# Two neighbouring rows of the second expert matrix in each partition, and the inner values turned in that order

## The chip, the cores and the metric

The kernel runs on one core of a Trainium2 chip. A core has TensorE (PE in the profile, with its weight loads counted apart as PEld), VectorE (DVE), ScalarE (ACT), GpSimd (POOL), SyncE (SP, which here only issues DMAs) and 16 DMA engines that move data between HBM and SBUF. The metric is the device time of one execution in microseconds (us). Before the change it is 1613.43 us, the median of 3 runs (1612.79 to 1615.95).

## The reference

One decoder block over 512 tokens of width 1024. A convolution mixer and a forgetting-attention mixer run side by side, then comes a mixture of 32 experts, of which each token takes 4. All weights are float32. The change touches the experts only; for one expert `e` and its block of up to 128 tokens `xi` the reference computes

```python
hc = xi @ w1[e] + b1[e]                       # w1[e]: 1024 x 2048
g, u = hc[:, :D_EXPERT], hc[:, D_EXPERT:]     # D_EXPERT = 1024
g = jnp.minimum(g, SWIGLU_LIMIT)
u = jnp.clip(u, -SWIGLU_LIMIT, SWIGLU_LIMIT)
hm = (u + 1.0) * (g * jax.nn.sigmoid(SWIGLU_ALPHA * g))   # the inner values
return hm @ w2[e] + b2[e]                     # w2[e]: 1024 x 1024
```

The product `hm @ w2[e]` is a sum over the 1024 inner values. The order in which they are taken is free, as long as `hm` and `w2` are taken in the same one.

## The kernel before

The first 480 us or so hold the mixers, the router and the ranking of the experts. Then the 32 experts are worked through in order of their token counts, in pairs: an even position `p` is a "big" expert (up to 128 rows of tokens), an odd one a "small" expert (up to 64 rows, `small(p)`, line 247). Each expert needs 8 tiles of `w1` and 4 of `w2`, and each tile is one DMA of 1 MB into 128 partitions of 8 KB, issued from SP in `slot` (lines 197 to 244). A `w1` tile is 128 rows of the matrix, one row of 8 KB to a partition (line 232). A `w2` tile is 256 rows of 4 KB, two to a partition (lines 238 to 240): partition `q` of tile `j` holds row `256*j + q` in its first half and row `256*j + 128 + q` in its second.

Seven buffers receive these tiles in turn (line 1079). A raw tile `w` is split into two float32r parts (`split`, line 1306): ACT copies it to `wh`, which rounds it, and DVE subtracts to give `wl`. Four buffers hold such parts, and `split_to` (line 1299) makes them up to three steps ahead of TensorE (`AHEAD`, line 37). A raw buffer is free for the next DMA when its `wl` has been made. Two of a small expert's eight `w1` tiles (`whole`, line 250) are used in float32 without a split.

The order of the work is written out in `steps` (line 1284): the `w1` tiles of expert `p` with the `w2` tiles of expert `p - 1` between them. While `pinned[0]` is set, every instruction of PE, ACT and DVE that goes through the wrappers of line 55 keeps the order of the program, so nearly all of them carry the line L55 and are told apart by their tiles.

For the second product `turn_h` (line 1235) turns the inner values `sg_u` (tokens in partitions) into `hmh` and `hml` (inner values in partitions). It makes 8 transposes on TensorE for each expert: a block of 128 columns of `sg_u` is loaded as the weights, and the identity is streamed past it, into the PSUM tile `pz`. ACT and DVE then split `pz`. In `mm_w2` (line 1352) block `kk = 2*k + cc` is the left operand for half `cc` of tile `k`, into the PSUM tile `py`:

```python
for cc in range(2):
    kk = 2 * k + cc
    for n in range(2):
        o = cc * D + n * 512
        MM(PSY[p][:, n * 512:n * 512 + 512], l[:, kk, :], r[:, o:o + 512],
```

For a small expert ACT copies the lower half of `py` into `b1s` when its last `w2` tile is done (`y_out`, line 1265), and TensorE adds it to the upper half with the matrix `shift` a little later (`y_low`, line 1269). The gates, the scatter into `x1d` and the final norm follow; the last expert has its own ending, with the bias rows (`bias_rows`, line 1387).

Of the kernel before, what the change touches and what calls it, by code (L numbers as in the profile page):

```python
# [19 lines left out]
P = 128  # L20
# [25 lines left out]
def hybrid_block(ctx, tc, x, c, w_ada, b_ada, norm1_g, w_in, b_forget, conv_w, conv_b, conv_ln_g,  # L46
# [5 lines left out]
    def in_order(f):  # L52

        def g(*args, **kw):
            ins = f(*args, **kw)  # L55
            return tc.keep_in_program_order(ins) if pinned[0] else ins
        return g

    MM = in_order(nc.tensor.matmul)
    TR = in_order(nc.tensor.transpose)  # L60
# [27 lines left out]
    def f32(ap):  # L88
        return ap.bitcast(F32)
# [4 lines left out]
    ident = K.tile([P, P], F32, name="ident")  # L94
# [86 lines left out]
    def raw_slot(dt=F32):  # L181
        t = pools[count[0] % len(pools)].tile([P, 2048], dt, name="w", tag="w")
        count[0] += 1
        return t
# [3 lines left out]
    def expert(p):  # L188

        if p == 0:  # L190
            return slice(0, 1)
        if p not in numbers:
            numbers[p] = nc.values_load(permi[0:1, p:p + 1], engines=[mybir.EngineType.SP], min_val=0, max_val=NE - 1,
                                        skip_runtime_bounds_check_because="an expert's number")
        return bass.ds(numbers[p], 1)

    def slot(*key):

        if key in slot_tiles:
            return slot_tiles[key]  # L200
        kind = key[0]
        dma = nc.sync.dma_start
        if kind == "ada" and key[1]:
            t = AD.tile([P, 2048], F32, name="adaw", tag="w")

            def dma(dst, src):
                tc.keep_in_program_order(nc.sync.dma_start(dst, src))
        else:
            t = raw_slot()
        if kind in COL:  # L210
            v = t.rearrange("p (c f) -> p c f", c=KC)
            c0 = COL[kind] + 256 * key[1]
            nc.sync.dma_start(v, w_in_v[:, :, c0:c0 + 256])
        elif kind == "ada":
            if key[1] < 2:
                v = t
                dma(v, w_ada[key[2] * P:(key[2] + 1) * P, 2048 * key[1]:2048 * (key[1] + 1)])
            else:
                v = t.rearrange("p (c f) -> p c f", c=2)
                dma(v, w_ada[2 * key[2] * P:2 * (key[2] + 1) * P, D * (key[1] + 2):D * (key[1] + 3)]  # L220
                    .rearrange("(c p) f -> p c f", p=P))
        elif kind in ("co", "ao"):
            src = (w_conv_out if kind == "co" else w_attn_out).rearrange("(c p) f -> p c f", p=P)
            v = t[:, :1024].rearrange("p (c f) -> p c f", c=4)
            nc.sync.dma_start(v, src[:, :, 256 * key[1]:256 * (key[1] + 1)])
        elif kind == "wo":
            v = t.rearrange("p (c f) -> p c f", c=4)
            nc.sync.dma_start(v, w_out[512 * key[2]:512 * (key[2] + 1), 512 * key[1]:512 * (key[1] + 1)]
                              .rearrange("(c p) f -> p c f", p=P))
        elif kind == "w1":  # L230
            v = t
            d = nc.sync.dma_start(v, w1[expert(key[1]), key[2] * P:(key[2] + 1) * P, :]
                                  .rearrange("o p f -> p (o f)"))
            if key[1] == 0 and key[2] >= 7:
                tc.keep_in_program_order(d)
        else:
            v = t
            d = nc.sync.dma_start(t.rearrange("p (c f) -> p c f", c=2),
                                  w2[expert(key[1]), 256 * key[2]:256 * (key[2] + 1)]
                                  .rearrange("o (c p) f -> p (o c) f", p=P))  # L240
            if key[1] == 0:
                tc.keep_in_program_order(d)
        slot_tiles[key] = v
        return v


    def small(p):
        return p % 2 == 1
# [11 lines left out]
    with ExitStack() as fx:  # L260
# [6 lines left out]
        def bank(name):  # L267
            return PS.tile([P, 512], F32, name=name, tag="b")
# [30 lines left out]
        def ada_acc(pc, k):  # L299
            w = slot("ada", pc, k)  # L300
            if pc > 1 and k == 0:
                acc[pc] = page([P, D], F32, "acc")
            for i in range(2):
                if pc < 2:
                    wi, o, kk, new = w[:, i * D:(i + 1) * D], acc[i], k, k == 0
                else:
                    wi, o, kk, new = w[:, i, :], acc[pc], 2 * k + i, k == 0 and i == 0
                if pc:
                    ACT(o if new else wi, wi, AF.Copy, scale=cs[:, kk:kk + 1])
                    if not new:  # L310
                        nc.gpsimd.tensor_tensor(o, o, wi, op=OP.add)  # L311
                elif new:
                    TS(o, wi, cs[:, kk:kk + 1], None, op0=OP.mult)
                else:
                    STT(o, wi, cs[:, kk:kk + 1], o, op0=OP.mult, op1=OP.add)
# [14 lines left out]
        def split_next():  # L330
            if not order:
                return
            key, half = order.pop(0)
            raw = slot(*key)[:, :, half * P:(half + 1) * P]
            kc = raw.shape[1]
            hi = G.tile([P, kc, P], F32R, name="gh", tag="gh")
            lo = G.tile([P, kc, P], F32R, name="gl", tag="gl")
            ACT(hi, raw, AF.Copy)
            TT(lo, raw, f32(hi), op=OP.subtract)
            ready[key, half] = (hi, lo)  # L340
# [155 lines left out]
        def split_v(hf):  # L496
            vh = pages(2, [P, 4, 260], F32R, "vh")
            vl = pages(2, [P, 4, 260], F32R, "vl")
            for q4 in range(2):
                ks = slice(4 * q4, 4 * q4 + 4)  # L500
                raw = slot("v", hf)[:, ks, :]
                fr = wf[:, ks, 4 * hf:4 * hf + 4]
                ACT(vh[q4][:, :, 256:260], fr, AF.Copy)
                TT(vl[q4][:, :, 256:260], fr, f32(vh[q4][:, :, 256:260]), op=OP.subtract)
                ACT(vh[q4][:, :, 0:256], raw, AF.Copy)
                TT(vl[q4][:, :, 0:256], raw, f32(vh[q4][:, :, 0:256]), op=OP.subtract)
            return vh, vl
# [27 lines left out]
        for hf in range(2):  # L535
            vh, vl = vs[hf]
            for b in range(NB):
                ts = slice(b * P, (b + 1) * P)
                ps = bank("pvv")
# [240 lines left out]
        def oproj(i, which, ah, al):  # L780
            hi, lo = split_of((which, i // 2), i % 2)
            ps = bank("po")
            run(three(ps, lambda k: hi[:, k, :], lambda k: lo[:, k, :],
                      lambda k: hk(ah, k), lambda k: hk(al, k), 4))
            return ps
# [102 lines left out]
        for i in range(KC):  # L888
# [3 lines left out]
            ps = oproj(i, "co", aH, aL)  # L892
# [179 lines left out]
    with ExitStack() as ex:  # L1072
# [110 lines left out]
        def rows(p):  # L1183
            return HALF if small(p) else P
# [34 lines left out]
        HT, HM, PSH, PSY = {}, {}, {}, {}  # L1219

        def swiglu(p):
# [10 lines left out]
            TS(u, u, LIMIT + 1.0, 1.0 - LIMIT, op0=OP.min, op1=OP.max)  # L1232
            STT(u, s, TOP, u, op0=OP.min, op1=OP.mult)

        def turn_h(p):


            r = rows(p)
            if small(p):
                if p < NE - 1:  # L1240
                    t = X.tile([P, KC, P], F32R, name="hmh", bufs=1)
                else:
                    t = G.tile([P, KC, P], F32R, name="hmh", tag="gh")
                ps = bank("pz")
                for k in range(KC):
                    TR(ps[:, k * r:(k + 1) * r], HM[p][:r, k * P:(k + 1) * P], ident[:r, :r])
                ps3 = ps.rearrange("p (k q) -> p k q", k=KC)
                ACT(t[:, :, 0:r], ps3, AF.Copy)
                TT(t[:, :, r:P], ps3, f32(t[:, :, 0:r]), op=OP.subtract)
                HT[p] = t  # L1250
                return
            hi = X.tile([P, KC, P], F32R, name="hmh", bufs=1)
            lo = X.tile([P, KC, P], F32R, name="hml", bufs=1)
            for hf in range(2):
                ps = bank("pz")
                for k in range(4):
                    kk = 4 * hf + k
                    TR(ps[:, k * P:(k + 1) * P], HM[p][:, kk * P:(kk + 1) * P], ident)
                ps3 = ps.rearrange("p (k q) -> p k q", k=4)
                ks = slice(4 * hf, 4 * hf + 4)  # L1260
                ACT(hi[:, ks, :], ps3, AF.Copy)
                TT(lo[:, ks, :], ps3, f32(hi[:, ks, :]), op=OP.subtract)
            HT[p] = (hi, lo)
# [182 lines left out]
        for i, (kind, p, k) in enumerate(steps):  # L1446
# [3 lines left out]
            if kind == "w1":  # L1450
# [35 lines left out]
                if k == 1 and p >= 1:  # L1486
                    turn_h(p - 1)
# [20 lines left out]
            else:  # L1508
# [13 lines left out]
                if (p, k) == (NE - 2, 3):  # L1522
                    turn_h(NE - 1)
# [204 lines left out]
```

## Time and profile before

| | |
|---|---|
| median of 3 runs | 1613.43 us (1612.79 to 1615.95) |
| profiled execution, its own time | 1611.79 us |
| its span | 1610.0 us |
| PE busy | 1488.9 us (92%) |
| DVE busy | 1349.4 us (84%) |
| ACT busy | 1043.4 us (65%) |
| DMA queue of SP (q1) | 461.93 MB, 72.9% of 16 engines |

The span runs from the first instruction to the last; the execution's own time is 1.79 us longer. Busy shares are means over stages with different limits, so the stage of the experts has to be read apart from the mixers. A row of waits gives the engine, what it was about to make, what it waited for, the total in us, how many times and the longest. An idle time in the timeline stands in brackets with what ended it.

### The profile page before, as it was taken

How to read it: one execution, taken by the hardware profiler on the slowest of the kernel's cores; microseconds unless marked ns; L12 is line 12 of the kernel's file. 1: busy time of each engine (PE TensorE's matmuls, PEld its weight loads, DVE VectorE, ACT ScalarE, POOL GpSimd, SP SyncE). 2: the span in 40 equal slices, each digit the busy share in tenths (PEclk: the TensorE clock that was granted, in tenths of full speed). 3: DMA queues.
4: the chain of work that ended last, by engine and by line, in shares of the span. 5: the costliest groups of instructions: out<-in, count | busy, mean ns of one | idle time of the engine just before them, and what ended most of it. 6: DMA issues, size and time to landing. Idle time of an engine off the chain costs nothing.

```text
span 1610.0 us, 18694 instructions
## 1 busy us (share of the span) xinstructions
PE 1488.9 (92%) x6626; PEld 1126.6 (70%) x6626; DVE 1349.4 (84%) x1282; ACT 1043.4 (65%) x953; POOL 406.6 (25%) x200
## 2 busy tenths in 40 slices
PE   2998999999967999999999999999999999999975
PEld 2776667778755777777777777777777777777743
DVE  6799998743676798898988989989898898988874
ACT  3534764522354777777777777877777777777671
POOL 0323341300131032231322313223222232222630
PEclk9997999989988999999999999999999999999987
DMA  8623342343557799999999999999999999999963
GB/s 321 208 79 105 103 132 99 124 144 95 206 196 258 312 362 400 389 407 406 394 392 407 390 404 368 404 384 408 389 391 393 399 390 402 385 386 373 405 243 114
DMA packets 115647, 489.81 MB, mean 304 GB/s; under 512 B 12983, under 2 KB 35627, under 8 KB 80728
## 3 DMA queue, kind: packets, MB, share of 16 engines
q1 hardware_dynamic: 103088, 461.93, 72.9%
q0 software_dynamic: 9200, 24.21, 5.4%
q10 hardware_dynamic: 3256, 2.39, 0.5%
q8 instruction: 54, 0.88, 0.2%
q14 instruction: 49, 0.40, 0.1%
HBM read 477.66 MB, written 18.63 MB: 308 GB/s over the span
## 4 chain that ended last, share of the span: by engine, by line
PE 55%; DVE 5%; ACT 4%; DMA 3%; issue 2%; POOL 0%; DVEq 0%; ACTq 0%
PE ph L55 37%; PE py L55 14%; DVE wl L55 3%; DMA w<-in_w_exp_in_dram 3%; ACT wh L55 3%; PE pz L55 2%; PE px L55 1%; ACT b1s L55 1%; ACT sg_u L55 1%; PE pi L55 1%; DMA xg<-in_b_exp_out_dram 0%; DVE w L55 0%; DVE sg_u L55 0%; DVE x L55 0%; DVE b1s L55 0%
## 5 line engine op out<-in xcount | busy, mean ns | idle before, releaser
L55 DVE TENSOR_TENSOR wl<-w,wh 128x2048 fp32r<-128x2048 f32 x352 | 796.5, 2282 | 89.5 <-ACT wh L55 86.2
L55 ACT ACTIVATE wh<-w 128x2048 fp32r<-128x2048 f32 x352 | 664.6, 1913 | 139.1 <-DMA w<-in_w_exp_out_dram 44.6
L55 PE MATMUL ph<-wh,xT 128*128 128x512 f32 x1408 | 377.0, 405 | 2.0 <-ACT sg_u L55 2.0
L55 PEld LDWEIGHTS ph<-wh,xT 128*128 128x128 f32 x1408 | 261.2, 190 | 72.3 <-issue 12.6
L1280 POOL DMA_INDIRECT x1d<-y,dstx x31 | 182.2, 5879 | 333.4 <-DVE y L55 333.4
L55 PE MATMUL ph<-wl,xT 128*128 128x512 f32 x896 | 241.6, 392 | 0.0
L55 PEld LDWEIGHTS ph<-wl,xT 128*128 128x128 f32 x896 | 169.1, 189 | 36.5
L55 PE MATMUL py<-wh,hmh 128*128 128x512 f32 x496 | 144.1, 412 | 1.3 <-DVE hmh L55 1.3
L55 PE MATMUL py<-wl,hmh 128*128 128x512 f32 x496 | 133.2, 390 | 0.2 <-DVE wl L55 0.2
L55 DVE SCALAR_TENSOR_TENSOR cacc<-apad,cw,cacc 128x512 f32<-128x512 f32 x120 | 117.3, 990 | 1.2
L55 PE MATMUL ph<-w,xT 128*128 128x512 f32 x256 | 115.2, 593 | 0.0
L311 POOL TENSOR_TENSOR acc<-acc,adaw 128x1024 f32<-128x1024 f32 x28 | 72.7, 2600 | 162.1 <-ACT adaw L55 156.2
L55 PEld LDWEIGHTS py<-wh,hmh 128*128 128x128 f32 x496 | 89.7, 188 | 31.9 <-issue 12.7
L55 PEld LDWEIGHTS py<-wl,hmh 128*128 128x128 f32 x496 | 93.0, 188 | 20.5 <-DVE wl L55 0.7
L55 ACT ACTIVATE gh<-w 128x1024 fp32r<-128x1024 f32 (+1 forms) x48 | 43.8, 914 | 87.6 <-PE zg L55 35.1
L1190 POOL MEMSET xg<- 64x1024 f32 (+1 forms) x31 | 29.6, 958 | 275.3 <-PE px L55 275.3
L1191 POOL DMA_INDIRECT xg<-h2d,dstx x31 | 65.6, 2116 | 117.5 <-DVE gat L55 103.0
L55 DVE TENSOR_TENSOR gl<-w,gh 128x1024 fp32r<-128x1024 f32 (+1 forms) x48 | 60.3, 1257 | 37.5 <-ACT gh L55 37.2
L55 PEld LDWEIGHTS ph<-w,xT 128*128 128x128 f32 x256 | 46.3, 190 | 46.1 <-issue 45.9
L55 ACT ACTIVATE xT<-px 128x512 fp32r<-128x512 f32 x50 | 29.7, 595 | 61.4 <-PE px L55 57.7
L55 PE MATMUL py<-wh,hml 128*128 128x512 f32 x256 | 68.6, 390 | 0.0
L55 ACT ACTIVATE sg_s<-ph 128x1024 f32<-128x1024 f32 (+1 forms) x32 | 32.8, 1024 | 44.3 <-PE ph L55 43.9
(379 smaller groups left out, 2106.6 us busy)
## 6 DMA issues: line engine op xcount, KB each, us to landing
w<-in_w_exp_in_dram SPq DMA_DIRECT2D x256, 1024.0 KB, 9.7
w<-in_w_exp_out_dram SPq DMA_DIRECT2D x128, 1024.0 KB, 12.4
w<-in_w_in_dram SPq DMA_DIRECT2D x18, 1024.0 KB, 5.6
adaw<-in_w_ada_dram SPq DMA_DIRECT2D x16, 1024.0 KB, 7.4
w<-in_w_ada_dram SPq DMA_DIRECT2D x8, 1024.0 KB, 6.8
w<-in_w_out_dram SPq DMA_DIRECT2D x4, 1024.0 KB
x<-in_x_dram SPq DMA_DIRECT2D x4, 512.0 KB
w<-in_w_attn_out_dram SPq DMA_DIRECT2D x4, 512.0 KB, 3.4
```

The costliest lines, as they stand in the source:

```text
L55: ins = f(*args, **kw)
L311: nc.gpsimd.tensor_tensor(o, o, wi, op=OP.add)
L1190: nc.gpsimd.memset(xgs[p][:r], 0.0)
L1191: nc.gpsimd.indirect_dma_start(out=xgs[p][:r], out_offset=None, in_=h2d[:, :], in_offset=bass.IndirectOffsetOnAxis(ap=dstx[:r, p:p + 1], a ...
L1280: nc.gpsimd.indirect_dma_start(out=x1d[:, :], out_offset=bass.IndirectOffsetOnAxis(ap=dstx[:r, p:p + 1], axis=0), in_=y, in_offset=None, b ...
```

## The change

A `w2` tile is read in another order: partition `q` of tile `j` now holds rows `256*j + 2*q` and `256*j + 2*q + 1`, which lie next to each other in HBM. The two pieces of 4 KB for a partition become one of 8 KB. So that the second product still pairs inner value and row, the block of `sg_u` that is turned as block `kk` is no longer 128 neighbouring columns but every second column of 256, starting at the even or the odd one.

```diff
@@ slot
             d = nc.sync.dma_start(t.rearrange("p (c f) -> p c f", c=2),
                                   w2[expert(key[1]), 256 * key[2]:256 * (key[2] + 1)]
-                                  .rearrange("o (c p) f -> p (o c) f", p=P))
+                                  .rearrange("o (p c) f -> p (o c) f", c=2))
@@ ahead of turn_h
+        def w2_rows(kk):
+
+            return slice(2 * P * (kk // 2) + kk % 2, 2 * P * (kk // 2 + 1), 2)
@@ turn_h, small expert
-                    TR(ps[:, k * r:(k + 1) * r], HM[p][:r, k * P:(k + 1) * P], ident[:r, :r])
+                    TR(ps[:, k * r:(k + 1) * r], HM[p][:r, w2_rows(k)], ident[:r, :r])
@@ turn_h, big expert
-                    TR(ps[:, k * P:(k + 1) * P], HM[p][:, kk * P:(kk + 1) * P], ident)
+                    TR(ps[:, k * P:(k + 1) * P], HM[p][:, w2_rows(kk)], ident)
```

No instruction is added or taken away, and none changes its place: PE, DVE, ACT, POOL and SP have the same instructions in the same order. On SP 127 rows of the listing read otherwise, the loads of `w2`, which have the form 128x2048 now (that of a `w1` load) where they had 128x2x1024.

## Rows read from the trace of the kernel before

**Rows 1.** The page: busy time of TensorE, the span in 40 slices with the granted clock and the DMA engines' share (tenths), and the count of DMA packets.

```profile
PE 1488.9 (92%) x6626; PEld 1126.6 (70%) x6626; DVE 1349.4 (84%) x1282; ACT 1043.4 (65%) x953; POOL 406.6 (25%) x200
...
PE   2998999999967999999999999999999999999975
...
PEclk9997999989988999999999999999999999999987
DMA  8623342343557799999999999999999999999963
...
DMA packets 115647, 489.81 MB, mean 304 GB/s; under 512 B 12983, under 2 KB 35627, under 8 KB 80728
```

**Rows 2.** Busy time of each engine in stretches of the stage of the experts (us from the span's start; busy us and number of instructions for PE, PEld, DVE, ACT, POOL; then the granted clock, the share of the DMA engines and GB/s).

```profile
600.00:700.00 100.00, 98.98 (x434) 74.83 (x434) 88.61 (x57) 76.83 (x53) 23.23 (x11) 1.00 1.00 396
700.00:800.00 100.00, 97.96 (x431) 73.18 (x430) 92.48 (x61) 74.99 (x52) 25.36 (x12) 1.00 1.01 400
...
1400.00:1500.00 100.00, 98.98 (x432) 74.32 (x431) 87.12 (x57) 76.62 (x53) 21.15 (x11) 1.00 0.97 384
```

**Rows 3.** Waits in the stretch from 600 to 1500 us: all of PE's, the DMA waits of ACT, and the longest of SP's queue.

```profile
PE py L55 <- ACT b1s L55: 13.2, 13, 1.0
...
ACT wh L55 <- DMA w<-in_w_exp_out_dram: 44.4, 34, 2.7
...
ACT wh L55 <- DMA w<-in_w_exp_in_dram: 24.7, 37, 2.3
...
SPq L232 <- DVE wl L55: 362.6, 154, 6.0
SPq L238 <- DVE wl L55: 144.0, 59, 3.1
```

**Rows 4.** The timeline from 719 us, around one of PE's waits (start, us, engine, line, operation, tiles, shape, count, idle time before).

```profile
719.25 1.03 ACT L55 ACTIVATE sg_s<-ph 128x1024 f32<-128x1024 f32 x1 [2.82 <-PE ph L55]
...
720.18 1.02 ACT L55 ACTIVATE sg_u<-ph 128x1024 f32<-128x1024 f32 x1
...
721.08 3.73 ACT L55 ACTIVATE wh<-w 128x2048 fp32r<-128x2048 f32 x2
...
724.83 1.02 ACT L55 ACTIVATE b1s<-py 64x1024 fp32r<-64x1024 f32 x1
...
725.90 0.73 PE L55 MATMUL py<-b1s,shift 64*128 64x512 f32 x2 [1.02 <-ACT b1s L55]
```

**Rows 5.** The page's median time from issue to landing of a tile of each matrix, and two stretches of 8 us, the first with loads of `w1` alone in flight, the second with loads of `w2` alone (columns as in Rows 2).

```profile
w<-in_w_exp_in_dram SPq DMA_DIRECT2D x256, 1024.0 KB, 9.7
w<-in_w_exp_out_dram SPq DMA_DIRECT2D x128, 1024.0 KB, 12.4
...
542.00:550.00 8.00, 8.00 (x37) 6.38 (x36) 5.23 (x4) 4.20 (x3) 0.96 (x1) 1.00 1.01 428
1539.00:1547.00 8.00, 8.00 (x30) 5.21 (x29) 8.00 (x5) 5.10 (x3) 8.00 (x1) 1.00 1.00 355
```

**Rows 6.** What SP spends on issuing one load, from 600 to 1500 us (ns, least, median and most; line 238 loads `w2`, line 232 `w1`).

```profile
L238 SPq DMA_DIRECT2D w<-in_w_exp_out_dram x108: 383/384/471, 599.9 to 1488.4; - x108
...
L232 SPq DMA_DIRECT2D w<-in_w_exp_in_dram x216: 332/333/690, 601.5 to 1499.1; - x108
```

**Rows 7.** Groups of weight loads on PE with their mean ns: those of the transposes of `sg_u` (the change is in these), those of the transposes of the tokens `xg`, one that loads 32 columns, one of an ordinary float32 product and the slowest of the list.

```profile
L55 PEld LDWEIGHTS pz<-ident,sg_u 128*128 128x128 f32 x128 | 14.9, 140 | 2.1
...
L55 PEld LDWEIGHTS pz<-ident,sg_u 64*128 64x128 f32 x128 | 9.5, 143 | 15.9 <-DVE sg_u L55 10.6 <-DVE y L55 4.9 <-issue 0.4
L55 PEld LDWEIGHTS px<-ident,xg 64*128 64x128 f32 x128 | 9.1, 139 | 5.3 <-issue 5.3
...
L55 PEld LDWEIGHTS pl<-wr,h2T 128*128 128x128 f32 x64 | 7.7, 191 | 4.9 <-ACT h2T L55 4.9
...
L55 PEld LDWEIGHTS pgo<-bdf,gT 128*128 128x128 f32 x2 | 0.5, 314 | 5.6 <-DVE bdf L55 5.6
...
L55 PEld LDWEIGHTS pq<-ident,CQ 128*32 128x32 f32 x4 | 0.4, 97 | 0.1
```

**Rows 8.** The timeline where a big expert's `sg_u` is turned (728 us) and a small one's (762 us): 8 weight loads and 8 transposes each; and the mean ns of one transpose of each kind.

```profile
728.52 1.03 PE L55 MATMUL pz<-ident,sg_u 128*128 128x128 f32 x8
...
762.23 0.57 PEld L55 LDWEIGHTS pz<-ident,sg_u 64*128 64x128 f32 x8 [0.35 <-DVE y L55]
762.23 0.71 PE L55 MATMUL pz<-ident,sg_u 64*128 64x64 f32 x8
...
L55 PE MATMUL pz<-ident,sg_u 128*128 128x128 f32 x128 | 16.6, 272 | 0.0
...
L55 PE MATMUL pz<-ident,sg_u 64*128 64x64 f32 x128 | 11.7, 234 | 10.2 <-DVE sg_u L55 10.2
```

**Rows 9.** The end of the stage: in the timeline a wait of DVE for the load of the bias rows and a wait of PE after it; then PE's longest wait after 1500 us.

```profile
1491.43 1.22 DVE L55 TENSOR_TENSOR xg<-xg,g2b 64x1024 f32<-64x1024 f32 x1 [3.05 <-DMA xg<-in_b_exp_out_dram]
...
1505.28 1.19 PE L55 MATMUL py<-wh,hmh 128*128 128x512 f32 x4 [1.26 <-DVE hmh L55]
...
PE pz L55 <- DVE sg_u L55: 10.2, 1, 10.2
```

## The prediction

> **What bounds the kernel now.** I read the page first. In its second part the PE line stands at 9 in every slice from the fifteenth to the thirty-eighth, with the clock at 9 tenths or more, and over the same slices the DMA line stands at 9 as well [rows 1]. So two resources look full at once, and the change relieves one of them. The question is which of the two sets the pace.
>
> The windows answer the first half: per 100 us of the stage PE is busy 97.96 to 98.98 us at a granted clock of 1.00, its 2.4 GHz level, while the DMA share is 0.97 to 1.01 [rows 2]. The waits answer the second half. From 600 to 1500 us PE waits for one thing only, 13 times, 13.2 us in all: `b1s`, a copy on ACT [rows 3]. That is about 1.02 us for each pair of experts. No wait of PE ends on a load or on a split. ACT does wait for loads, 44.4 us for `w2` tiles and 24.7 for `w1` tiles in these 900 us [rows 3], but the split runs up to three tiles ahead of PE, and that lead swallows these waits. SP in its turn holds back loads until DVE has emptied a buffer, 362.6 and 144.0 us [rows 3]: the loads are asked for at the pace at which tiles are used. A DMA share near 1 then means that there is always something in flight, not that more is wanted.
>
> The one wait has nothing to do with loads either. At 719.25 ACT, which had been idle 2.82 us for PE's `ph`, makes `sg_s`, then `sg_u`, two `wh`, then `b1s`, without a gap up to 725.85, and PE goes on at 725.90 [rows 4]. What starts this run is PE's own `ph`. The pace of the stage is that of PE.
>
> **The loads.** The new `w2` load has the shape of a `w1` load, so the trace already prices it. From issue to landing a `w2` tile takes 12.4 us, a `w1` tile 9.7 [rows 5]. With only `w2` in flight the engines moved 355 GB/s, with only `w1` 428, both at a share of 1.00 or 1.01 [rows 5]. A tile of 1.0486 MB is 2.95 us at the one rate and 2.45 at the other, so at most 0.50 us x 128 tiles = 64 us of DMA time is set free. The stretch of 355 GB/s lies in the ending, with other work about, so I take 64 as an upper end and 0 as the lower one. On the clock this counts 0: its cover is PE, which has no wait for a load that could shrink [rows 3]. What it does shorten is ACT's 44.4 us of waiting, behind which PE still works on tiles made earlier. If the cover were gone, the most that could be won is all of PE's idle time in the stage, 1.02 us x 16 pairs = 16 us, since the products themselves stay.
>
> SP needs 384 ns to issue a `w2` load and 333 for a `w1` load [rows 6], so 51 ns x 128 = 6.5 us of SP's time go. SP's 507 us of waiting for buffers lie over that: 0 on the path. What is late next is unchanged, DVE's release of the buffer.
>
> Packets, as a check of the form: 128 tiles of 256 packets become 128 of 128, so the page's 115647 should fall by 16384 to 99263, and "under 8 KB" from 80728 by 32768 to 47960. That `w1` goes in packets of 8 KB shows in the same row: 115647 - 80728 = 34919 are that large, and 256 `w1` tiles of 128 make 32768 [rows 1].
>
> **The ending.** DVE waits 3.05 us for the bias rows until 1491.43 us; their load shares the DMA engines with weight loads. At 1505.28 PE has waited 1.26 us for `hmh`, which DVE makes [rows 9]. Faster loads could take between 0 and 1.3 us out of it; I take 0.5. PE's 10.2 us wait for the last `sg_u` [rows 9] ends on DVE and stays.
>
> **The turned blocks.** This is the part that can cost, for it is on PE, which has nothing to hide it. 32 experts x 8 = 256 weight loads now read every second float32 of 256 columns in place of 128 neighbours. The trace has no weight load of such a step. Its bounds: a load follows the number of columns it brings (97 ns for 32 columns, 140 for 128 [rows 7]), and that number stays, so it can hardly become cheaper, 0 on that side. On the other side the nearest row of the same shape that is slower is a float32 load for an ordinary product, 191 ns against 140 [rows 7]: 51 ns more. The farthest is 314 ns [rows 7], 174 ns more. Fully exposed that gives 256 x 51 ns = 13.1 us, and 256 x 174 ns = 44.5 us at the far end.
>
> How much would be exposed differs by kind. For a small expert the 8 loads start every (0.57 - 0.143)/7 = 61 ns and its transposes every (0.71 - 0.234)/7 = 68 ns [rows 8]: the load is the pace, and every ns added is paid, 8 x 51 = 0.41 us. For a big one the transposes start every (1.03 - 0.272)/7 = 108 ns [rows 8]; a load of 61 + 51 = 112 ns would show by 4 ns seven times and once in full, 0.08 us. Over 16 pairs that is 16 x 0.49 = 7.8 us.
>
> I take 0, the row nearest in kind: the loads for `pz` and `px` of the same shape take 139 to 143 ns whichever tile they read [rows 7], one column each 0.4 ns or so ((140 - 97)/96), and a step that doubles the distance is not a new column. This is a choice, and the 7.8 us stay in the range.
>
> The Trainium skill speaks to this in SBUF — State Buffer, Specifications (TRN2): SBUF is read by lines of 16 bytes, and an access pattern keeps full bandwidth with two or more hits to a line. Every second float32 is two hits to a line, the last step that is still free by that rule, and by it the term is 0. The same row says that each crossing to a new line pays a penalty, which speaks against the change: 128 values now cross 64 lines in place of 32. No row here shows a strided weight load, so this trace bears out neither half.
>
> **Sum.** The profiled execution took 1611.8 us, its span 1610.0. Loads 0, SP 0, turned blocks 0, ending -0.5: 1611.3. The median of the runs is 1.6 above that execution, so on its scale about 1613.
>
> **Rivals.**
> - Slower, by the strided weight loads: each of the 256 loads takes 51 ns longer, as the 191 ns row does. 7.8 us, so 1621; fully exposed 13.1, so 1626.5, and 1658 by the farthest row. It decides from about 22 ns a load on (3.2 us / 144, the 128 loads of small experts and the first of each big one). For it: PE is full and the small experts' transposes go at the pace of their loads. Against it: the same number of columns, and no row in which the place of the data changed the time of a load.
> - Faster, by the loads: DMA is the true limit and PE merely keeps up. Then up to PE's whole idle time goes, 16 us, and 1597 is the floor; half of it, 8 us, gives 1605. For it: a DMA share of 1.00 and 69 us of ACT's waits. Against it: none of PE's waits ends on a load, and the one that exists starts from PE itself.
> - The change does not do what it says: the 8 KB are cut into two packets of 4 KB again. Then 1613 too, and only the count of packets tells it. Against it: `w1` loads of this form already go as 8 KB.
>
> **How the numbers follow.** No strided cost 0.71 (0.01 of it for loads that stay cut), strided cost 0.21 (0.15 near 8 us, 0.06 above 13), faster by the loads 0.08. About 0.2%, 3.2 us, is what a measurement can tell here; the three runs of before lie within that. Within the first case 0.65 stays in that bound, 0.04 falls below and 0.02 above it; the second is slower but for 0.01, the third faster but for 0.01. Together faster 0.11, same 0.67, slower 0.22. The range of 1608 to 1623 holds the first case and the near half of the second, with room for a spread of 2 us; it leaves out the costs above 13 us and most of the case of faster loads.
>
> **What would show it.** Right: 99263 packets; landing of `w2` near 9.7 us; ACT's wait for `w2` well under 44 us; loads for `pz` still at 139 to 143 ns beside `px`, which is not touched; PE's wait for `b1s` still 1.02 us a pair. The rival of the loads shows as PE waits or idle time gone; the strided rival as `pz` loads above 140 ns with `px` at 139, and 8 small transposes that take more than 0.71 us. The forecast falls if the stage from 600 to 1500 us changes its length by more than 3 us.

## The result and the profile after

The changed kernel takes 1622.26 us, the median of 6 runs (1620.26 to 1623.04). The kernel before, run beside it, takes 1613.11 us (1611.75 to 1615.95). The ratio is 1.0052 with a 95% interval of 1.0040 to 1.0065: 9.15 us slower. The profiled execution took 1620.26 us, its span 1618.5.

The page of the changed kernel first: busy time by engine, the packets, and the median time from issue to landing of a tile of each matrix.

```profile
PE 1504.9 (93%) x6626; PEld 1142.6 (71%) x6626; DVE 1347.1 (83%) x1282; ACT 1042.7 (64%) x953; POOL 406.8 (25%) x200
...
DMA packets 99263, 489.81 MB, mean 303 GB/s; under 512 B 12983, under 2 KB 35627, under 8 KB 47960
...
w<-in_w_exp_in_dram SPq DMA_DIRECT2D x256, 1024.0 KB, 8.9
w<-in_w_exp_out_dram SPq DMA_DIRECT2D x128, 1024.0 KB, 11.6
```

The packets are exactly those of 8 KB loads, and both kinds of tile land 0.8 us sooner than in [rows 5]. PE has 16.0 us more of busy time than in [rows 1]; 7.8 us of that lie in the first 600 us, where the granted clock differs (from 400 to 480 us it is 0.86, in the kernel before 0.93). The waits between 600 and 1500 us, of PE and of ACT:

```profile
PE py L55 <- ACT b1s L55: 13.2, 13, 1.0
...
ACT wh L55 <- DMA w<-in_w_exp_out_dram: 26.1, 20, 2.2
...
ACT wh L55 <- DMA w<-in_w_exp_in_dram: 19.6, 22, 2.4
```

PE's one wait is what it was in [rows 3], to the tenth. ACT waits less for loads, and the kernel is slower all the same. The groups of weight loads, with the untouched transposes of the tokens (`px`) for comparison:

```profile
L55 PEld LDWEIGHTS pz<-ident,sg_u 128*128 128x128 f32 x128 | 17.8, 206 | 1.3
...
L55 PEld LDWEIGHTS pz<-ident,sg_u 64*128 64x128 f32 x128 | 16.5, 212 | 16.0 <-DVE sg_u L55 11.1 <-DVE y L55 4.9
L55 PEld LDWEIGHTS px<-ident,xg 128*128 128x128 f32 x120 | 14.9, 139 | 3.9
...
L55 PEld LDWEIGHTS px<-ident,xg 64*128 64x128 f32 x128 | 9.1, 139 | 5.3 <-issue 5.3
```

A load for `pz` takes 206 and 212 ns where [rows 7] has 140 and 143; `px` stands at 139. No strided load escapes: here are the least, median and most of all loads for `pz` between 600 and 1500 us, first in the kernel before, then in the changed one. So the blocks that start at an even column pay like those that start at an odd one.

```profile
L55 PEld LDWEIGHTS pz<-ident,sg_u x216: 135/139/143, 628.6 to 1498.1; 64*128 64x128 f32 x56, 128*128 128x128 f32 x52
```

```profile
L55 PEld LDWEIGHTS pz<-ident,sg_u x208: 192/209/215, 628.1 to 1471.2; 64*128 64x128 f32 x52, 128*128 128x128 f32 x52
```

In the timeline the 8 transposes of a big expert (729 us) and of a small one (762 us), and the use of `b1s` at two places that lie 13 pairs of experts apart:

```profile
591.63 0.73 PE L55 MATMUL py<-b1s,shift 64*128 64x512 f32 x2 [1.02 <-ACT b1s L55]
...
729.09 1.11 PE L55 MATMUL pz<-ident,sg_u 128*128 128x128 f32 x8
...
762.93 1.03 PEld L55 LDWEIGHTS pz<-ident,sg_u 64*128 64x128 f32 x8 [0.35 <-DVE y L55]
762.93 1.17 PE L55 MATMUL pz<-ident,sg_u 64*128 64x64 f32 x8
...
1467.88 0.73 PE L55 MATMUL py<-b1s,shift 64*128 64x512 f32 x2 [1.01 <-ACT b1s L55]
```

The same use of `b1s` in the timeline of the kernel before:

```profile
592.21 0.72 PE L55 MATMUL py<-b1s,shift 64*128 64x512 f32 x2 [1.01 <-ACT b1s L55]
...
1461.27 0.73 PE L55 MATMUL py<-b1s,shift 64*128 64x512 f32 x2 [1.02 <-ACT b1s L55]
```

Against [rows 8] the small expert's transposes take 1.17 - 0.71 = 0.46 us more and the big one's 1.11 - 1.03 = 0.08, together 0.54 us a pair. A pair takes (1467.88 - 591.63)/13 = 67.40 us after and (1461.27 - 592.21)/13 = 66.85 before: 0.55 us more. Over 16 pairs that is 8.8 of the 9.15 us. The transposes account for the longer pair to 0.01 us, so nothing else on PE's path in the pair moved.

### The profile page after: what moved, and what is told of

It is laid out like the page before. It is cut to its first block, busy times and chain, and to the rows that moved or that the text cites. A ratio compares the mean times of both kernels' runs of the same rounds, so it can differ in the third digit from the quotient of the medians.

```text
span 1618.5 us, 18694 instructions
## 1 busy us (share of the span) xinstructions
PE 1504.9 (93%) x6626; PEld 1142.6 (71%) x6626; DVE 1347.1 (83%) x1282; ACT 1042.7 (64%) x953; POOL 406.8 (25%) x200
## 2 busy tenths in 40 slices
DMA packets 99263, 489.81 MB, mean 303 GB/s; under 512 B 12983, under 2 KB 35627, under 8 KB 47960
## 4 chain that ended last, share of the span: by engine, by line
PE 56%; DVE 5%; ACT 4%; DMA 3%; issue 3%; ACTq 0%; DVEq 0%
PE ph L55 37%; PE py L55 15%; DVE wl L55 3%; DMA w<-in_w_exp_in_dram 3%; ACT wh L55 2%; PE pz L55 2%; PE px L55 1%; ACT b1s L55 1%; ACT sg_u L55 1%; PE pi L55 1%; DVE w L55 0%; DVE x L55 0%; DVE b1s L55 0%; DVE pis L55 0%; DVE sg_u L55 0%
## 5 line engine op out<-in xcount | busy, mean ns | idle before, releaser
L55 PEld LDWEIGHTS py<-wh,hmh 128*128 128x128 f32 x496 | 89.7, 188 | 32.3 <-issue 13.2
L55 ACT ACTIVATE sg_s<-ph 128x1024 f32<-128x1024 f32 (+1 forms) x32 | 32.8, 1024 | 44.3 <-PE ph L55 44.0
## 6 DMA issues: line engine op xcount, KB each, us to landing
w<-in_w_exp_out_dram SPq DMA_DIRECT2D x128, 1024.0 KB, 11.6
```

## The experiments

Eleven kernels were run, seven timed repeatedly beside the kernel before, four in a single run. Six of them (the turn alone, the loads alone, the other steps, the ordinary products) multiply values and rows that do not belong together, and so compute another product of the same size. As long as the joining stays where it is, the pair of experts is the better measure: the first use of `b1s` lies anywhere from 589.95 to 596.00 us in these traces, while at a granted clock of 1.00 the 13 pairs of one trace are even (66.83 to 66.87 us before, 67.37 to 67.44 after).

**The turn alone.** The old loads with the new turn.

```diff
-                                  .rearrange("o (p c) f -> p (o c) f", c=2))
+                                  .rearrange("o (c p) f -> p (o c) f", p=P))
```

> The old loads of w2 (two pieces of 4 KB to a partition) with the new, strided turn of the inner values; inner values and rows no longer match, so the output is another product of the same size. Theory S (the strided weight loads of the transposes are the whole loss): slower than before by 9 us, ratio 1.004 to 1.007, weight loads for pz at 206 to 212 ns, a pair of experts at 67.4 us. Theory L (the 8 KB loads cost or give part of it): clearly off that, under 1.003 if the loads are half of the loss, over 1.008 if they give time back.

Measured: 1619.47 us beside 1612.74, ratio 1.0045 (1.0032 to 1.0058). Its groups of weight loads and its timeline:

```profile
L55 PEld LDWEIGHTS pz<-ident,sg_u 128*128 128x128 f32 x128 | 17.8, 206 | 1.4
...
L55 PEld LDWEIGHTS pz<-ident,sg_u 64*128 64x128 f32 x128 | 16.5, 211 | 15.9 <-DVE sg_u L55 10.6 <-DVE y L55 4.9 <-issue 0.4
```

```profile
591.77 0.73 PE L55 MATMUL py<-b1s,shift 64*128 64x512 f32 x2 [1.02 <-ACT b1s L55]
...
1468.31 0.73 PE L55 MATMUL py<-b1s,shift 64*128 64x512 f32 x2 [1.02 <-ACT b1s L55]
```

The loads have the length that they have in the changed kernel, and a pair takes (1468.31 - 591.77)/13 = 67.43 us. The turn alone brings the whole loss of a pair. The median is 6.7 us slower, 2.3 us short of the expected 9; 9 us (1.0056) still lies in the interval.

**The loads alone.** The new loads with the old turn.

```diff
-            return slice(2 * P * (kk // 2) + kk % 2, 2 * P * (kk // 2 + 1), 2)
+            return slice(kk * P, (kk + 1) * P)
```

> The new loads of w2 (8 KB to a partition) with the old turn of neighbouring columns; inner values and rows do not match, so the output is another product of the same size. Theory S: the loads are hidden, within 0.2% of before (1610 to 1616 us), weight loads for pz at 140 ns, a pair at 66.85 us, ACT's wait for w2 tiles between 600 and 1500 us under 30 us in place of 44. Theory L: 4 us or more off before, to either side.

Measured: 1613.97 us beside 1612.74, ratio 1.0013 (1.0004 to 1.0023). From its timeline, and the wait of ACT for `w2` between 600 and 1500 us:

```profile
589.95 0.72 PE L55 MATMUL py<-b1s,shift 64*128 64x512 f32 x2 [1.01 <-ACT b1s L55]
...
1459.06 0.73 PE L55 MATMUL py<-b1s,shift 64*128 64x512 f32 x2 [1.02 <-ACT b1s L55]
```

```profile
ACT wh L55 <- DMA w<-in_w_exp_out_dram: 39.2, 28, 2.2
```

A pair takes (1459.06 - 589.95)/13 = 66.85 us, that of before to the hundredth. So the loads neither give nor cost in the stage. The interval lies just above 1, by at most 0.23%; the next kernel has the same loads and does not show it, so where those 1 to 2 us would be stays open. One expectation was missed: ACT's wait fell from 44.4 to 39.2 us only, not under 30. The turn alone has 39.6 us there, so neither half by itself brings the 26.1 us of the changed kernel. With the old loads and the turn at step 3, 4 and 8 (below) the wait is 28.8, 33.0 and 39.6 us: it varies by as much as is to be explained, and what makes it so short in the changed kernel stays open.

**The order made on ACT.** The new loads and the old turn; the two activations that read PSUM put the values in the new order, which keeps inner value and row together.

```diff
-            ACT(s, ph[:, :FE], AF.Gelu_apprx_sigmoid)
-            ACT(u, ph[:, FE:], AF.Identity, bias=1.0)
+            def turned(t):
+                return t.rearrange("r (j q c) -> r j c q", j=4, c=2)
+
+            def blocks(t):
+                return t.rearrange("r (j c q) -> r j c q", j=4, c=2)
+
+            ACT(blocks(s), turned(ph[:, :FE]), AF.Gelu_apprx_sigmoid)
+            ACT(blocks(u), turned(ph[:, FE:]), AF.Identity, bias=1.0)
```

> The new loads, the old turn of neighbouring columns, and the order is made on ACT: the two activations that make sg_s and sg_u read PSUM at every second value and write blocks. Theory S: weight loads for pz back at 140 ns and, if the two activations keep their 1.03 us, the time of before (1610 to 1616 us). Rival: ACT pays for the step; with 1.03 us more for each of the two, PE's wait for b1s grows by 2 us a pair and the time by up to 33 us.

Measured: 1612.98 us beside 1612.74, ratio 1.0003 (0.9990 to 1.0016). The two activations of this kernel between 600 and 1500 us (ns, least, median and most), and a small expert's transposes:

```profile
L55 ACT ACTIVATE sg_u<-ph x27: 1007/1011/1022, 623.2 to 1492.5; 64x1024 f32<-64x1024 f32 x14, 128x1024 f32<-128x1024 f32 x13
```

```profile
L55 ACT ACTIVATE sg_s<-ph x27: 1017/1022/1030, 622.3 to 1491.5; 64x1024 f32<-64x1024 f32 x14, 128x1024 f32<-128x1024 f32 x13
```

```profile
763.66 0.57 PEld L55 LDWEIGHTS pz<-ident,sg_u 64*128 64x128 f32 x8 [0.35 <-DVE y L55]
763.66 0.71 PE L55 MATMUL pz<-ident,sg_u 64*128 64x64 f32 x8
```

ACT reads every second float32 of PSUM at the 1.02 us of [rows 4], and the transposes are those of [rows 8] again. The use of `b1s` moves from 593.57 to 1462.86 us, so a pair takes 66.87 us. The same order of values costs 9 us as a stride of the weight loads and nothing that shows as a stride of the activations. It wins nothing over the kernel before either.

**Other steps of the turn.** One run each, with the old loads: every fourth, every eighth and every third column.

```diff
-            return slice(2 * P * (kk // 2) + kk % 2, 2 * P * (kk // 2 + 1), 2)
+            return slice(4 * P * (kk // 4) + kk % 4, 4 * P * (kk // 4 + 1), 4)
```

> The old loads, and a turn that reads every fourth column of 512 (another product of the same size). Theory of lines (the cost follows the number of 16-byte lines that the 128 values touch: 32 at step 1, 64 at step 2, 128 at step 4): weight loads for pz clearly above those of step 2, small transposes every 240 ns in place of 120, the time about 1645 us. Theory of a lost fast path (any step but 1 costs the same): 206 to 212 ns, 120 ns apart, 1622 us.

```diff
+            return slice(kk, 8 * P, 8)
```

> The old loads, and a turn that reads every eighth column of 1024 (another product of the same size). Theory of lines: as at step 4, since 128 values already touch 128 lines there, small transposes about 240 ns apart. Theory of a lost fast path: as at step 2, 120 ns apart. If the cost follows the distance itself, twice that of step 4.

```diff
+            return slice(kk * 88, kk * 88 + 3 * P - 2, 3)
```

> The old loads, and a turn that reads every third column (another product of the same size). If any step but 1 falls back to the pace of an ordinary float32 weight load, small transposes stand 110 to 120 ns apart and the loads take 189 to 212 ns, as at 2, 4 and 8. If the cost came from the lines touched, the same at this step as at 4 and 8; what tells here is whether it is 120 (as at 2 and 4) or 110 (as at 8).

Measured: 1619.61, 1623.21 and 1621.34 us, single runs. A small expert's 8 loads and transposes in the timeline, at step 4:

```profile
764.32 1.03 PEld L55 LDWEIGHTS pz<-ident,sg_u 64*128 64x128 f32 x8 [0.35 <-DVE y L55]
764.33 1.17 PE L55 MATMUL pz<-ident,sg_u 64*128 64x64 f32 x8
```

At step 8:

```profile
766.87 0.96 PEld L55 LDWEIGHTS pz<-ident,sg_u 64*128 64x128 f32 x8 [0.35 <-DVE y L55]
766.88 1.09 PE L55 MATMUL pz<-ident,sg_u 64*128 64x64 f32 x8
```

At step 3:

```profile
766.07 0.99 PEld L55 LDWEIGHTS pz<-ident,sg_u 64*128 64x128 f32 x8 [0.35 <-DVE y L55]
766.07 1.13 PE L55 MATMUL pz<-ident,sg_u 64*128 64x64 f32 x8
```

The 8 transposes take 1.17 us at steps 2 and 4, 1.13 at 3 and 1.09 at 8, against 0.71 at step 1. The cost does not grow with the distance, nor with the lines touched, by which step 4 would cost more than step 2. Most of it, 0.38 of 0.46 us, is paid at each of these steps. (The totals of single runs do not rank them, since the start of the stage shifts by more than they differ. The pairs do: from the use of `b1s` at 593.06 and 1469.48 us at step 4, 594.97 and 1470.43 at step 3, 596.00 and 1470.37 at step 8, a pair takes 67.42, 67.34 and 67.26 us, the same order as the transposes.) The step of an ordinary float32 weight load is near that level: in the kernel before, 8 loads of `h2T` in a row,

```profile
428.47 0.97 PEld L55 LDWEIGHTS pl<-wr,h2T 128*128 128x128 f32 x8 [0.93 <-ACT h2T L55]
```

start every (0.97 - 0.19)/7 = 111 ns, with 191 ns for the last from [rows 7]. At steps 2 and 4 the loads start every 117 ns, at step 3 every (0.99 - 0.205)/7 = 112 and at step 8 every (0.96 - 0.199)/7 = 109. Why they differ was not tried.

**Ordinary products with a step.** The kernel before, with the left operand of the small experts' first product read at every second column.

```diff
+            if small(p):
+                flat = XT[p].rearrange("p k q -> p (k q)")
+                xs = flat[:, 2 * P * (k // 2) + k % 2:2 * P * (k // 2 + 1):2]
             if whole(p, k):
-                calls = ((f32(XT[p][:, k, :]), hi),)
+                calls = ((f32(xs), hi),)
             elif small(p):
-                xs = XT[p][:, k, :]
```

> The kernel before, but in the first product of the small experts the left operand is read at every second column (another product of the same size): weight loads of ordinary float32r and float32 products at step 2. If only the transposes have a faster load to lose, those loads keep their 188 to 190 ns and the time stays at 1613. If every strided load pays, they take some 255 ns, and the time grows where they do not lie beside a product of 227 ns.

Measured: 1618.92 us in a single run. Its groups of weight loads (all 256 of `ph<-w,xT` are at the step, those of `ph<-wh,xT` only where the expert is small), its window from 700 us, and the use of `b1s` at two places 8 pairs apart:

```profile
L55 PEld LDWEIGHTS ph<-wh,xT 128*128 128x128 f32 x1408 | 263.8, 192 | 71.3 <-issue 12.4 <-ACT sg_u L55 7.1
...
L55 PEld LDWEIGHTS ph<-w,xT 128*128 128x128 f32 x256 | 47.9, 196 | 44.9 <-issue 44.7
```

```profile
700.00:800.00 100.00, 97.71 (x425) 74.08 (x424) 90.31 (x60) 74.62 (x51) 25.90 (x11) 0.98 1.01 393
```

```profile
931.08 0.73 PE L55 MATMUL py<-b1s,shift 64*128 64x512 f32 x2 [0.95 <-ACT b1s L55]
...
1467.55 0.74 PE L55 MATMUL py<-b1s,shift 64*128 64x512 f32 x2 [0.96 <-ACT b1s L55]
```

That was expected at 188 to 190 or at 255 ns and came out at 196 for the float32 loads, 6 ns above the 190 of the kernel before. So an ordinary load pays 6 ns where a transposing one pays 66. But it is not free, and the time did not stay at 1613: in the pairs from 931 us on, where the granted clock is 1.00 as in [rows 2], a pair takes (1467.55 - 931.08)/8 = 67.06 us, 0.21 more than before, or 3.4 us over 16 pairs. The granted clock is 0.98 in the window from 700 us, so another part of the 1618.9 us is not the step's; the rest was not followed up.

**The joining later.** If PE sets the pace, taking away its one wait should show. The kernel before, with `y_low` and `finish` one `w1` tile later:

```diff
-                if k == 0 and p >= 2 and small(p - 2):
+                if k == 1 and p >= 2 and small(p - 2):
```

> The kernel before, with TensorE's use of b1s (the joining of a small expert's lower half) and the finish behind it put one w1 tile later. Theory that PE sets the pace of the stage: its only wait there, 1.02 us a pair, goes and the time falls by about 15 us to 1598, with nothing in its place. Rival, the DMA engines set the pace: the time stays within 4 us of 1613 and PE waits for wh or wl in place of b1s.

> The 8 KB loads with the order made on ACT, and the joining one w1 tile later. If PE sets the pace and ACT's activations keep their 1.03 us: like the run with the joining alone, 1598 us, within 3 us of it. If the loads of 4 KB limit the kernel once PE's wait is gone: 3 us or more faster than that run. If ACT pays for the step: slower than that run by what the two activations grow.

Measured: 1610.76 us, ratio 0.9986 (0.9971 to 1.0001), and with the 8 KB loads and the order made on ACT 1608.75 us, ratio 0.9970 (0.9960 to 0.9981), both beside 1613.5. PE's waits between 600 and 1500 us in the first of the two:

```profile
PE py L55 <- DVE y L55: 7.6, 9, 1.3
PE ph L55 <- DVE wl L55: 1.2, 1, 1.2
```

In the second:

```profile
PE py L55 <- DVE y L55: 4.1, 7, 1.6
PE ph L55 <- DVE wl L55: 1.9, 1, 1.9
```

The wait for `b1s` is gone, and part of its 13.2 us came back in another place, 8.8 us in the first kernel and 6.0 in the second: DVE, in the order of the program, makes `y` behind a `wl` that waits for a load. The expected 15 us were 2.7, with an interval that just reaches 1, and 4.8.

**The joining ahead of the next split.** As above, and in that step the split of the next tiles comes behind the joining.

```diff
-            split_to(i)
+            joins = kind == "w1" and k == 1 and p >= 2 and small(p - 2)
+            if not joins:
+                split_to(i)
             if kind == "w1":
                 mm_w1(p, k)
-                if k == 0 and p >= 2 and small(p - 2):
+                if joins:
                     y_low(p - 2)
                     finish(p - 2)
+                    split_to(i)
```

> The kernel before with the joining one w1 tile later, and in that one step the split of the next tiles comes behind the joining and the finish, so that DVE's y no longer stands behind a wl that waits for a load. Theory that PE sets the pace and the wait for y in the run with the joining alone came from that order: PE's waits between 600 and 1500 us fall under 3 us, the time to about 1600 (13 us off). Rival, the loads set the pace as soon as PE's own wait is gone: PE then waits for wh or wl, the time stays over 1606.

> The same with the 8 KB loads and the order made on ACT. If the loads are still hidden, the time of the run before it (h), within 3 us. If the loads of 4 KB hold that run back, 3 us or more faster than it.

Measured: 1608.69 us, ratio 0.9974 (0.9962 to 0.9986), and with the 8 KB loads and the order on ACT 1604.98 us, ratio 0.9957 (0.9943 to 0.9971), both beside 1613.93. The first is not at the 1600 that were expected, and PE's waits in it add up to 6.9 us, not to under 3. The rival fits no better: the time stays over 1606, but PE waits for `wl` once, 1.3 us, and not for `wh`. The largest wait of PE and that of ACT for `w2`, then those of the second:

```profile
PE py L55 <- DVE hml L55: 5.3, 8, 0.9
...
ACT wh L55 <- DMA w<-in_w_exp_out_dram: 58.6, 53, 1.9
```

```profile
PE py L55 <- DVE hml L55: 2.4, 5, 0.6
...
ACT wh L55 <- DMA w<-in_w_exp_out_dram: 53.2, 48, 1.8
```

With PE's own wait away, what it waits for most is DVE's `hml`, and ACT waits longer for loads than in [rows 3]. Here the larger packets may begin to count. The use of `b1s` lies in the first kernel at

```profile
595.48 0.73 PE L55 MATMUL py<-b1s,shift 64*128 64x512 f32 x2
...
1458.31 0.73 PE L55 MATMUL py<-b1s,shift 64*128 64x512 f32 x2
```

and in the second at

```profile
591.71 0.72 PE L55 MATMUL py<-b1s,shift 64*128 64x512 f32 x2
...
1450.85 0.73 PE L55 MATMUL py<-b1s,shift 64*128 64x512 f32 x2
```

so that a pair takes 862.83/13 = 66.37 and 859.14/13 = 66.09 us on average. The gain of 0.28 us a pair (4.5 us over 16) agrees with the medians (3.7 us); between the two kernels of the later joining it is 0.28 us a pair as well (66.57 and 66.30 us), with medians 2.0 us apart. But without the wait for `b1s` the pairs are uneven, from 65.66 to 66.96 us in the first kernel and from 65.67 to 66.65 in the second, and the intervals of each two kernels overlap: a gain is likely, not settled. The order on ACT goes with the larger packets here, and the two were not run apart. The shortest pair, 65.66 us, is about what PE needs when nothing holds it up (in the first kernel it is busy for all of the 100 us from 600). The last kernel beats both the kernel before, by 8.95 us, and the changed one.

## Why the prediction was wrong

- The step that failed is the value chosen for the turned blocks: "I take 0, the row nearest in kind". The experiment with the turn alone shows that term as the whole loss. A strided transposing load takes 206 to 212 ns, not 140. The argument that a load follows the number of its columns held for loads at step 1, the only ones that the prediction's rows had, and was stretched to a step that none of them showed.
- The rule cited beside it, two hits to a 16-byte line for full bandwidth (the Trainium skill, SBUF — State Buffer, Specifications (TRN2)), does not hold for these loads: step 2 has two hits and pays in full. Nor does its other half, a penalty for each line crossed, give the size: step 4 crosses twice as many and pays no more.
- The rival of strided loads had place and mechanism right. Its terms were 51 ns a load, 0.41 us for a small and 0.08 us for a big expert, 7.8 us in all; measured were 66 to 69 ns, 0.46 and 0.08 us, 8.8 us over the pairs. That the big expert's 0.08 us agrees is luck: it was to be 4 ns seven times and one load in full, and it came as 10 ns seven times (transposes every (1.11 - 0.281)/7 = 118 ns for 108, with 0.281 us for the last) and 9 ns on the last. The median of 1622.26 us lies beyond the 1621 of that case and within the range given, but the forecast was no change, at odds of 0.67 to 0.22. A cost that no row shows, on the engine that sets the pace, deserved more than the 0.21 it got.
- Loads at 0: right. The loads alone leave a pair at 66.85 us. That PE sets the pace of the stage: right for this kernel, with its wait for `b1s` unchanged at 13.2 us. But the margin was thin. The floor of 1597 for a stage without that wait is not reached by removing it: of the 1.02 us a pair, 66.85 - 66.37 = 0.48 were won with the old loads, since PE then waits for DVE, while ACT waits longer for loads.
- Packets: 99263 and 47960, as worked out. SP's issue of a `w2` load fell to 333 ns. Landing came down to 11.6 us rather than 9.7: the `w1` tiles came down too, and the distance between the two kinds stayed at 2.7 us. With the order made on ACT it is 12.4 us for the same 8 KB loads, and at step 3 of the turn 11.7 with the old ones, so it is not a matter of packets. The rates that the prediction took from [rows 5] do not bear it out either: from 1547 to 1555 us, in the ending with `w2` all but alone in flight, the kernel with the turn alone moves 396 GB/s in packets of 4 KB, where the kernel before had 355, and the changed kernel 356 in packets of 8. So the `w1` loads did not price the new `w2` loads, and the runs do not show the 64 us of DMA time; the 0 on the clock did not rest on them.
- The ending: no gain of 0.5 us seen; DVE's wait for the bias rows was 3.9 us there in place of 3.05.

## What to carry to other kernels

When a change of layout moves a stride from a DMA to an operand, ask which engine gets it and whether that engine sets the pace: here the stride cost 0.54 us a pair on TensorE's transposes and nothing on ACT, which reads PSUM anyway. An operation that the trace shows only in one form has no price in another form; until it is measured, the nearest slower row is the estimate, not the fastest. And a stream that is full without being waited for gives nothing when its packets are made larger, as long as the engine in front of it sets the pace.

## What the hardware showed that was not expected

- A float32 transpose's weight load of 128 columns runs at one every 61 ns when the columns are neighbours, and at one every (1.03 - 0.212)/7 = 117 ns at step 2 and 4, near the 111 ns of an ordinary float32 load. That the transposing load has a faster form for neighbouring columns, which any step loses, is a reading that fits steps 2, 3, 4 and 8; what that form consists of was not tried.
- An ordinary weight load at step 2 takes 196 ns for 190, and a float32 activation of 1024 values that reads PSUM at step 2 takes the same 1.02 us as one that reads neighbours.
